# A hybrid RWKV-7 / gated-DeltaNet block: triangular inverses transposed into their own tile, the last of their loads requested first, and scan operands in longer DRAM pieces

## The chip, the core and the metric

One NeuronCore of a Trainium2 chip runs the whole two-layer network in one launch. The time is what the device takes for one execution, in microseconds (us). The kernel before took 3481.66 us (median of three runs, 3479.96 to 3486.83). The engines are called as in the profile: PE (TensorE matmul), PEld (its weight load), DVE (VectorE), ACT (ScalarE), POOL (GpSimd) and SP (SyncE). SP computes nothing in this kernel; it issues nearly all loads, one after the other.

## The reference

Float32 throughout. Layer 0 mixes tokens with two recurrences, each run forward and backward over 256 context and 1024 latent tokens:

```python
def _rwkv_scan(state0, r, decay, k, v, kk, b):      # 8 heads of 64
    def step(state, inp):
        r_t, w_t, k_t, v_t, kk_t, b_t = inp
        sa = jnp.einsum('bhij,bhj->bhi', state, kk_t)
        state = (state * w_t[:, :, None, :] - sa[..., None] * b_t[:, :, None, :]
                 + v_t[..., None] * k_t[:, :, None, :])
        return state, jnp.einsum('bhij,bhj->bhi', state, r_t)
...
def _gdn_chunked(state0, q, k, v, g, beta):         # 4 heads of 128, chunks of 64
    l_mat = jnp.where(strict, jnp.einsum('nbhid,nbhjd->nbhij', k_beta, kc) * decay, 0.0)
    sol = lax.linalg.triangular_solve(l_mat, rhs, left_side=True, lower=True, unit_diagonal=True)
    a_intra = jnp.where(incl, jnp.einsum('nbhid,nbhjd->nbhij', qc, kc) * decay, 0.0)
    def step(state, inp):
        q_i, k_i, u_i, w_i, g_i, a_i = inp
        v_new = u_i - jnp.einsum('bhlk,bhkv->bhlv', w_i, state)
        ...
```

Then come the output projection, an expert-choice mixture of experts, a layer of windowed attention, a second mixture of experts and a norm. The change touches the two recurrences and what prepares them.

## The kernel before, in words

Both recurrences are computed in 20 chunks of 64 tokens (`NCH`), two directions at once, by the same method: within a chunk a 64x64 unit lower triangular matrix is inverted, and a state is carried from chunk to chunk. There are 12 units: 0 to 3 are RWKV head pairs forward, 4 to 7 backward, 8 to 11 the DeltaNet heads.

**Preparation.** `InProj.run` multiplies the tokens by the input weights, one 128-column block after another. Each block's weights (`wraw`, two buffers) come through SP and are split into a high and a low part by ACT and POOL (`wlo`). Between the matmuls generators are stepped that prepare the operands. `Rwkv.prep_gen` forms, per block of 256 or 512 tokens and direction, the decayed arrays alpha, rho, beta and kappa in tile `arbk` and stores them as `s_rk`; `chunk_L` multiplies them to the triangular matrices and stores `s_L`; `vt` is the value array (`s_v`). `Gdn` does the same with a convolution (`convu`, DVE line L702), normalised k and q (`kqn` and `kqf`, stored as `s_kq`), decay matrices (`la`, stored as `s_L` and `s_At`) and token rows (`tok`, stored as `s_kv`). All these stores are issued by POOL. The order of these instructions on each engine is made by a scheduler that follows priorities; the generators of the inverses get a raised one (`tfill`).

**Inverses.** `tri_inv` loads 32x32 diagonal blocks into tile `invB`, one block per partition, and runs 31 elimination steps of two DVE instructions each (L852 `invt`, L853 `invX`). ACT writes the transpose into another tile, `invXT`, of the same two buffers, and both forms are stored as `s_T`. Eight such chains run one after the other. The seventh (96 partitions: the later chunks of unit 9 and the first four of units 10 and 11) ends the preparation, and the scan cannot form its first corner before it is stored. The eighth (units 10 and 11, chunks 4 to 19) runs inside the scan.

**Scan.** `Scan.run` has one step per chunk n. Here PE, DVE and POOL follow the order in which the code is written (`ORDER`): `rwkv` (ps_u, ps_U, ps_S, state S), `gdn` (ps_ks, ps_qs, ps_Y, ps_Sg), `corner(n+1)` (ps_p: the off-diagonal 32x32 corner of each inverse, from the tiles `t1`, `TT` and `l21`) and `gram(n+1)`. The loads are `load2` once per two chunks (tiles ar, bk, kq in both directions: 14 DMAs on SP), `load_tri(n+2)` (l21, t1 and four parts of TT: 6 DMAs) at the head of step n, and `load_tok(n+2)` (sv 4, at 1, and a gather of kv on POOL) at its end. SP works them off in that order. At the end of step 6 (`LATER`) `load_raw` requests the output weights `wo_raw`, 8 DMAs of 512 KB. Chain 8 is stepped once per letter of `ORDER`, so it fills DVE in steps 0 and 1.

The runs of consecutive bytes in the DRAM arrays are short: ar, the second half of bk and sv are loaded in pieces of 256 bytes, the first half of bk and kq in pieces of 512, and t1, TT and l21 in pieces of 128. The row of at is already one piece of 1 KB.

## Time and profile before

| | before |
|---|---|
| median of three runs | 3481.66 us |
| the profiled execution | 3488.81 us |
| its span, first to last instruction | 3487.0 us |
| mean granted TensorE clock | 0.945 of full speed |
| busy in the span: PE, DVE, ACT, POOL | 3127.7, 2438.2, 2074.6, 726.7 us |

The profiled execution is 7.15 us above the median, and 1.8 us of it lie outside the span. Shares over the whole span say little about this change: it touches the stretch from about 180 us (the first `arbk`) to 1224 us (the last output of the scan). The preparation's last projection matmul ends at about 807 us; the scan's steps run from about 842 to 1224 us. A wait row names the instruction that waited and what released it; an SP row gives when a DMA was issued and how long the issue held SP.

### The profile page before, as it was taken

To read this page: it belongs to the slowest core of one execution; us is meant where nothing else is said; L and a number is where in the kernel's file an instruction comes from. 1 tells how busy PE (TensorE), PEld (TensorE's weight loads), DVE (VectorE), ACT (ScalarE), POOL (GpSimd) and SP (SyncE) were. 2 spreads that over 40 slices of the span, in tenths; PEclk is the share of its full clock that TensorE was granted. 3 is DMA by queue.
4 is the path that set the end of the run, shared out by engine and by line. 5 is a ranking of instruction groups with operands and counts; after the bars stand their busy time and mean duration, and the time that the engine had idled before them with its cause. 6 is when DMAs were issued, how large, how long until landed. Compare 5 with 4: busy or idle time off the path is not lost. (4 is left out here: it accounts for less than half of the span.)

```text
span 3487.0 us, 60267 instructions
## 1 busy us (share of the span) xinstructions
PE 3127.7 (90%) x23392; PEld 2393.5 (69%) x23392; DVE 2438.2 (70%) x4066; ACT 2074.6 (59%) x3548; POOL 726.7 (21%) x716
## 2 busy tenths in 40 slices
PE   5999899995879878699999999799699958999997
PEld 3866667775768757567666767467577746888885
DVE  4268884666534457877777777634876787999998
ACT  4255454332434455477777667534688838888886
POOL 1133332222333343201111110011233310010101
PEclk9999999897889989799999999899899979999998
DMA  5256656666999765578888887662311058999995
GB/s 194 75 181 197 191 194 201 204 187 123 202 221 199 169 218 169 187 254 298 299 286 282 307 287 283 221 212 95 83 49 49 34 205 303 395 384 392 386 380 208
DMA packets 480161, 767.80 MB, mean 220 GB/s; under 512 B 231836, under 2 KB 318532, under 8 KB 472708
## 3 DMA queue, kind: packets, MB, share of 16 engines
q1 hardware_dynamic: 434640, 601.05, 51.5%
q0 software_dynamic: 41648, 151.55, 13.9%
q10 hardware_dynamic: 3587, 11.36, 1.1%
q8 instruction: 184, 3.01, 0.4%
q14 instruction: 102, 0.83, 0.1%
HBM read 631.48 MB, written 132.38 MB: 219 GB/s over the span
## 5 line engine op out<-in xcount | busy, mean ns | idle before, releaser
L1223 DVE TENSOR_TENSOR ulo<-raw,uhi 128x1024 fp32r<-128x1024 f32 x768 | 898.0, 1219 | 84.1 <-ACT uhi L1222 69.7
L1222 ACT ACTIVATE uhi<-raw 128x1024 fp32r<-128x1024 f32 x768 | 790.6, 1073 | 196.6 <-PE ps_y L1662 89.2
L1611 PE MATMUL ps_h<-uhi,xh 128*128 128x512 f32 x1024 | 329.0, 399 | 2.1 <-ACT uhi L1222 2.0
L1611 PE MATMUL ps_h<-ulo,xh 128*128 128x512 f32 x1024 | 319.3, 392 | 3.7 <-DVE ulo L1223 3.0
L1611 PE MATMUL ps_h<-uhi,xl 128*128 128x512 f32 x1024 | 318.6, 392 | 0.0
L1678 POOL DMA_INDIRECT s_x<-yo,idxl x31 | 49.2, 1588 | 945.0 <-DVE yo L1674 945.0
L1611 PEld LDWEIGHTS ps_h<-ulo,xh 128*128 128x128 f32 x1024 | 190.4, 188 | 53.9 <-DVE ulo L1223 12.7
L1611 PEld LDWEIGHTS ps_h<-uhi,xh 128*128 128x128 f32 x1024 | 186.2, 188 | 51.0 <-ACT uhi L1222 8.7
L1611 PEld LDWEIGHTS ps_h<-uhi,xl 128*128 128x128 f32 x1024 | 191.2, 188 | 40.6
L354 PE MATMUL ps_in<-hl,whi 128*128 128x512 f32 x512 | 173.0, 411 | 0.0
L354 PE MATMUL ps_in<-hh,whi 128*128 128x512 f32 x512 | 172.4, 413 | 0.0
L354 PE MATMUL ps_in<-hh,wlo 128*128 128x512 f32 x512 | 171.9, 410 | 0.0
L1662 PE MATMUL ps_y<-uhi,th 128*128 128x512 f32 x512 | 162.1, 397 | 0.7 <-ACT tc L1648 0.6
L1662 PE MATMUL ps_y<-ulo,th 128*128 128x512 f32 x512 | 159.9, 393 | 0.1
L1662 PE MATMUL ps_y<-uhi,tl 128*128 128x512 f32 x512 | 158.1, 390 | 0.0
L1584 ACT ACTIVATE xv<-ps_x,Gf 128x128 f32<-128x128 f32 x256 | 96.9, 471 | 67.0 <-PE ps_x L1580 67.0
L1962 POOL TENSOR_SCALAR pe<-pe,ast 128x640 f32<-128x640 f32 (+1 forms) x48 | 90.2, 1879 | 185.9 <-DVE ast L1961 88.0
L1976 PE MATMUL ps_pT<-ident,pe 128*128 128x128 f32 x608 | 95.9, 282 | 35.1 <-ACT pT L1980 17.2
L852 DVE TENSOR_TENSOR invt<-invB,invX 128x112 f32<-128x112 f32 (+27 forms) x248 | 102.0, 411 | 29.9 <-DMA invB<-s_L 24.6
L1662 PEld LDWEIGHTS ps_y<-uhi,th 128*128 128x128 f32 x512 | 93.7, 188 | 38.9 <-ACT uhi L1222 12.0
L1949 DVE CUSTOM_DVE_ANT_0 pe<-ps_s,amask,sink 128x640 f32<-128x640 f32 (+2 forms) x128 | 103.4, 809 | 24.2 <-PE ps_s L1942 22.8
L1617 PE MATMUL ps_hc<-raw,xc 128*32 128x512 f32 x1024 | 119.6, 596 | 0.0
(505 smaller groups left out, 7276.7 us busy)
## 6 DMA issues: line engine op xcount, KB each, us to landing
raw<-in_moe_w_dram SPq DMA_DIRECT2D x384, 1024.0 KB
ada_w<-in_ada_w_dram SPq DMA_DIRECT2D x48, 1024.0 KB
wraw<-in_e_w_in_dram SPq DMA_DIRECT2D x32, 512.0 KB
s_rk<-arbk POOLq DMA_DIRECT2D x16, 1024.0 KB, 5.2
kq<-s_kq SPq DMA_DIRECT2D x20, 512.0 KB
s_x<-ox POOLq DMA_DIRECT2D x18, 512.0 KB, 3.0
s_h<-ot POOLq DMA_DIRECT2D x18, 512.0 KB, 3.9
s_rkv<-rkv POOLq DMA_DIRECT2D x12, 640.0 KB, 3.9
```

The costliest lines, as they stand in the source:

```text
L354: nc.tensor.matmul(ps, l[:, k, :], r[:, k, a:a + m], start=(k == 0 and n == 0), stop=(k == 7 and n == 2))
L852: nc.vector.tensor_mul(t, B[:N, k, k + 1:, None].to_broadcast([N, r, c]), X[:N, k, None, 0:c].to_broadcast([N, r, c]))
L1222: K.nc.scalar.activation(hi, src, AF.Copy)
L1223: K.nc.vector.tensor_sub(lo, src, hi)
L1584: nc.scalar.activation(v[:, q], pt[:, q], AF.Identity, bias=self.nrm[:, 1, k, 0:1], scale=self.nrm[:, 0, k, 0:1])
L1611: nc.tensor.matmul(pl[m][n], l[:, k], r[:, 512 * n:512 * n + 512], start=(k == 0 and i == 0), stop=(k == 7 and i == 2))
L1617: nc.tensor.matmul(pc[32 * g:32 * g + 32], xc[:, k_], rs[g // 2][:, 512 * (g % 2):512 * (g % 2) + 512], start=(k_ == 0), stop=(k_ == 7), s ...
L1662: nc.tensor.matmul(py[n], l[:, k], r[:, 512 * n:512 * n + 512], start=(k == 0 and i == 0), stop=(k == 7 and i == 2))
L1678: nc.gpsimd.indirect_dma_start(out=K.s_x[1], out_offset=bass.IndirectOffsetOnAxis(ap=idx[:, e:e + 1], axis=0), in_=yo, in_offset=None, com ...
L1949: nc.vector.tensor_tensor_reduce(pe[:, a:b], sc[:, 512 - nl + a:512 - nl + b], self.mask[:, m:m + b - a], 1.0, low, OP.add, OP.min, st[:, ...
L1962: (nc.vector if n < NV else nc.gpsimd).tensor_scalar(pes[0][:, :nk], pes[0][:, :nk], st[:, 4, 0:1], None, op0=OP.mult)
L1976: nc.tensor.transpose(pt[:, k, i_], pes[i_][:, 128 * (c + k):128 * (c + k) + 128], K.ident)
```

## The change

- `tri_inv`: the transpose goes into the chain's own `invB` tile (`XT = B`) and no longer into a second buffer, so the next chain's `invB` has the other buffer.
- The eighth chain's generator is stepped once before `Scan` is built, so its `invB` loads stand ahead of all scan loads; `run` then steps it once where it stepped it twice.
- `s_rk` becomes (10, 128, 4, 512), with alpha and rho of two chunks first and beta and kappa after them: ar loads in pieces of 512 bytes, the first half of bk in pieces of 1 KB, the second half stays at 256 bytes. `s_kq` becomes (10, 128, 4, 2, 128): kq loads in pieces of 4 KB, and is stored with 16 DMAs in pieces of 512 bytes where it was 8 in pieces of 10 KB. `s_v` is ordered by head parity: sv loads with 2 DMAs in pieces of 1 KB where it was 4, and is stored with 24 DMAs in pieces of 256 bytes where it was 12 in pieces of 512. DVE forms kd first and then turns `av` in place into (av + 1) kk; the count of its instructions is unchanged.
- `wo_raw`: one of its 8 DMAs at the end of each of the steps 6 to 13.

```diff
@@ -539,22 +540,28 @@
-                x = wk.tile([128, 8, 4, 64], F32, name="arbk", tag="arbk", bufs=2)
+                x = wk.tile([128, 4, 512], F32, name="arbk", tag="arbk", bufs=2)
...
-                    return ap.rearrange("p (c t) -> p c t", t=64)
-                al, rh, be, ka = (x[:, :n, i] for i in range(4))
-                nc.vector.scalar_tensor_tensor(be, N3(av[:, :m]), 1.0, N3(kk[:, :m]), op0=OP.add, op1=OP.mult)
-                nc.vector.tensor_scalar(av[:, :m], av[:, :m], P("ka", ct), self.tka[:, ct:ct + 1],
+                    return ap.rearrange("p (m c t) -> p m c t", c=2, t=64)
...
+                def E4(sl):
+                    return E[:, :n, sl].rearrange("p (m c) t -> p m c t", c=2)
...
+                x1, x2 = (x[:, :n // 2, i:i + 256] for i in (0, 256))
+                al, rh = (x1.rearrange("p m (s c t) -> p m s c t", c=2, t=64)[:, :, i] for i in range(2))
+                be, ka = (x2.rearrange("p m (c s t) -> p m s c t", c=2, t=64)[:, :, i] for i in range(2))
+                kd = wk.tile([128, 512], F32, name="kd", tag="kd", bufs=2)
+                nc.vector.tensor_scalar(kd[:, :m], av[:, :m], P("ka", ct), self.tka[:, ct:ct + 1],
...
-                kd = wk.tile([128, 512], F32, name="kd", tag="kd", bufs=2)
-                nc.vector.tensor_mul(kd[:, :m], av[:, :m], k)
+                nc.vector.tensor_mul(kd[:, :m], kd[:, :m], k)
+                nc.vector.scalar_tensor_tensor(av[:, :m], av[:, :m], 1.0, kk[:, :m], op0=OP.add, op1=OP.mult)
...
-                nc.vector.tensor_mul(al, E[:, :n, exc], N3(kk[:, :m]))
-                nc.vector.tensor_mul(be, be, N3(iE[:, :m]))
-                nc.vector.tensor_mul(rh, E[:, :n, inc], N3(r))
+                nc.vector.tensor_mul(al, E4(exc), N3(kk[:, :m]))
+                nc.vector.tensor_mul(be, N3(av[:, :m]), N3(iE[:, :m]))
+                nc.vector.tensor_mul(rh, E4(inc), N3(r))
@@ -562,8 +569,8 @@
-                                    x[:, :n].rearrange("p (m c) s t -> p m (c s t)", c=2))
+                                    x[:, :n // 2])
@@ -592,8 +599,9 @@
-            nc.gpsimd.dma_start(dap(K.s_v, a * 512 + ct * 128, [[512, 128], [128 * 512, q], [1, 128]]),
-                                vt.rearrange("p (q i) -> p q i", i=128)[:, :q])
+            for h in range(2):
+                nc.gpsimd.dma_start(dap(K.s_v, a * 512 + h * 256 + ct * 64, [[512, 128], [128 * 512, q], [1, 64]]),
+                                    vt.rearrange("p (q h i) -> p h q i", h=2, i=64)[:, h, :q])
@@ -726,7 +734,9 @@
-                    nc.gpsimd.dma_start(dap(K.s_kq[d], h * 2 * T, [[8 * T, 128], [1, 2 * T]]), x.rearrange("p s t -> p (s t)"))
+                    for q in range(2):
+                        nc.gpsimd.dma_start(dap(K.s_kq[d], h * 256 + q * 128, [[1024, 128], [128 * 1024, 10], [1, 128]]),
+                                            x[:, q].rearrange("p (m t) -> p m t", t=128))
@@ -852,7 +862,7 @@
-    XT = wk.tile([128, 32, 32], F32, name="invXT", tag="invB", bufs=bufs)
+    XT = B
@@ -925,18 +935,20 @@
-            def v(p0, np_, arr, n=64):
-                return dap(K.s_rk[d], (mm * 128 + p0) * 2048 + arr * 64, [[2048, np_], [256, 8], [1, n]])
+            def v(p0, np_, o, n):
+                return dap(K.s_rk[d], (mm * 128 + p0) * 2048 + o, [[2048, np_], [512, 4], [1, n]])
...
-                return x.rearrange("p c k t -> p (c k) t")
-            nc.sync.dma_start(w(ar[0:64, 0]), v(0, 64, 0))
-            nc.sync.dma_start(w(ar[64:128, 1]), v(64, 64, 0))
-            nc.sync.dma_start(w(ar[:, 2]), v(0, 128, 1))
-            nc.sync.dma_start(bk[0:64].rearrange("p c k s t -> p (c k) (s t)"), v(0, 64, 2, 128))
+                return x.rearrange("p c k t -> p c (k t)")
+            nc.sync.dma_start(w(ar[0:64, 0]), v(0, 64, 0, 128))
+            nc.sync.dma_start(w(ar[64:128, 1]), v(64, 64, 0, 128))
+            nc.sync.dma_start(w(ar[:, 2]), v(0, 128, 128, 128))
+            nc.sync.dma_start(bk[0:64].rearrange("p c k s t -> p c (k s t)"), v(0, 64, 256, 256))
...
-                nc.sync.dma_start(w(bk[64:128, :, :, s]), v(64, 64, 3 - s))
-            nc.sync.dma_start(kq.rearrange("p h s t -> p (h s) t"), dap(K.s_kq[d], m * 128, [[8 * T, 128], [T, 8], [1, 128]]))
+                nc.sync.dma_start(bk[64:128, :, :, s].rearrange("p c k t -> p (c k) t"),
+                                  dap(K.s_rk[d], (mm * 128 + 64) * 2048 + 256 + 64 * (1 - s),
+                                      [[2048, 64], [512, 4], [128, 2], [1, 64]]))
+            nc.sync.dma_start(kq.rearrange("p h s t -> p (h s t)"), dap(K.s_kq[d], m * 128 * 1024, [[1024, 128], [1, 1024]]))
@@ -962,14 +974,13 @@
-            for d in range(2):
-                m = step_of(n) if d else n
-                nc.sync.dma_start(sv[r, hp, 4 * d:4 * d + 4], dap(K.s_v, 64 * m * 512 + hp * 64, [[512, 64], [128, 4], [1, 64]]))
+            nc.sync.dma_start(sv[r, hp].rearrange("p (d c) t -> p d (c t)", d=2),
+                              dap(K.s_v, 64 * n * 512 + hp * 256, [[512, 64], [64 * 512 * (step_of(n) - n), 2], [1, 256]]))
@@ -1181,7 +1192,7 @@
-        tri.step(2)
+        tri.step()
@@ -1206,8 +1217,8 @@
-            if n == LATER:
-                later(self.last)
+            if LATER <= n < LATER + 8:
+                later(n - LATER, self.last)
@@ -1323,10 +1334,9 @@
-def load_raw(K, t, W, last):
...
-    for k in range(8):
-        behind(K, K.nc.sync.dma_start(t[:, k], rows_ap(W, 128 * k * D, 128, D)), last.ins.name)
+def load_raw(K, t, W, k, last):
...
+    behind(K, K.nc.sync.dma_start(t[:, k], rows_ap(W, 128 * k * D, 128, D)), last.ins.name)
@@ -2126,11 +2136,11 @@
-        K.s_rk = [dt(f"s_rk{d}", (10, 128, 4, 2, 4, 64)) for d in range(2)]
+        K.s_rk = [dt(f"s_rk{d}", (10, 128, 4, 512)) for d in range(2)]
...
-        K.s_kq = [dt(f"s_kq{d}", (128, 4, 2, T)) for d in range(2)]
+        K.s_kq = [dt(f"s_kq{d}", (T // 128, 128, 4, 2, 128)) for d in range(2)]
@@ -2193,7 +2203,8 @@
-                Scan(K, sp, psg, psr, psn).run(lambda x: load_raw(K, wo, A["e_w_out"], x), tri)
+                tri.step()
+                Scan(K, sp, psg, psr, psn).run(lambda k, x: load_raw(K, wo, A["e_w_out"], k, x), tri)
```

SP at the change from preparation to scan, before: the loads of chunks 0 and 1 (sv, at, l, t, TT) and, behind them, chain 8's `invB`.

```order
L967 DMA sv<-s_v 64x4x64 x4
L972 DMA at<-s_At 128x256
L948 DMA l_6632<-s_L 128x12x32
L951 DMA t_6633<-s_T_165 128x12x32
L955 DMA TT_6635<-s_T_165 32x12x32 x4
L967 DMA sv<-s_v 64x4x64 x4
L972 DMA at<-s_At 128x256
L948 DMA l_6658<-s_L 128x12x32
L951 DMA t_6659<-s_T_165 128x12x32
L955 DMA TT_6661<-s_T_165 32x12x32 x4
L841 DMA invB<-s_L 32x32x32 x4
L948 DMA l_6847<-s_L 128x12x32
```

The same queue after, where the scan's loads begin; `wraw` and `ada_w` are weight loads of the preparation.

```order
L186 DMA ada_w<-in_ada_w_dram 128x2048 x5
L851 DMA invB<-s_L 8x32x32 x2
L186 DMA ada_w<-in_ada_w_dram 128x2048
L327 DMA wraw<-in_e_w_in_dram 128x8x128 x2
L851 DMA invB<-s_L 8x32x32 x2
L851 DMA invB<-s_L 32x32x32 x4
L943 DMA ar_6621<-s_rk_152 64x4x128
L944 DMA ar_6621<-s_rk_152 64x4x128
L945 DMA ar_6621<-s_rk_152 128x4x128
```

Chain 8's loads (32x32x32 x4) now stand ahead of the first ar load. Chain 7's (the 8x32x32 rows, and one 32x32x32 row further up) are spread between the weight loads; before, all six stood behind the last of these.

DVE near the end of the preparation, before: the last convolution (L702) among the steps of chain 7. The last number of L852 is the step's size, which rises to 256 at the middle of a chain and falls to 31 at its end.

```order
L702 SCALAR_TENSOR_TENSOR convu<-ps_inc,prm,convu 128x254
L853 TENSOR_TENSOR invX<-invX,invt 96x19x13
L702 SCALAR_TENSOR_TENSOR convu<-ps_in,prm,convu 128x1022
L852 TENSOR_TENSOR invt<-invB,invX 96x252
L702 SCALAR_TENSOR_TENSOR convu<-ps_in,prm,convu 128x1023
L853 TENSOR_TENSOR invX<-invX,invt 96x18x14
L702 SCALAR_TENSOR_TENSOR convu<-ps_in,prm,convu 128x1023
L852 TENSOR_TENSOR invt<-invB,invX 96x255
L702 SCALAR_TENSOR_TENSOR convu<-ps_in,prm,convu 128x1022
L853 TENSOR_TENSOR invX<-invX,invt 96x17x15
L852 TENSOR_TENSOR invt<-invB,invX 96x256
```

The same convolution after (L710), with what follows it up to the scan's first DVE instruction (L1012, in the old file L1001).

```order
L710 SCALAR_TENSOR_TENSOR convu<-ps_inc,prm,convu 128x254
L862 TENSOR_TENSOR invt<-invB,invX 96x60
L710 SCALAR_TENSOR_TENSOR convu<-ps_in,prm,convu 128x1022
L863 TENSOR_TENSOR invX<-invX,invt 96x2x30
L710 SCALAR_TENSOR_TENSOR convu<-ps_in,prm,convu 128x1023
L862 TENSOR_TENSOR invt<-invB,invX 96x31
L710 SCALAR_TENSOR_TENSOR convu<-ps_in,prm,convu 128x1023
L863 TENSOR_TENSOR invX<-invX,invt 96x31
L710 SCALAR_TENSOR_TENSOR convu<-ps_in,prm,convu 128x1022
L781 TENSOR_TENSOR tok<-ps_tk,vsc 128x512 x2
L781 TENSOR_TENSOR tok<-ps_tk,vsc 128x256
L1012 TENSOR_TENSOR ar_6621<-ps_g,strict 64x4x64
```

Before, chain 7 is at its middle when the last convolution ends, and 30 of its instructions follow before L1001; now the chain ends among the convolution's instructions, and only tok stands between them and the scan.

SP at step 6 of the scan, before, and then after.

```order
L972 DMA at<-s_At 128x256
L1329 DMA wo_raw<-in_e_w_out_dram 128x1024 x8
L948 DMA l_8910<-s_L 128x12x32
L951 DMA t_8911<-s_T_166 128x12x32
L955 DMA TT_6635<-s_T_166 32x12x32 x4
L967 DMA sv<-s_v 64x4x64 x4
L972 DMA at<-s_At 128x256
L948 DMA l_9193<-s_L 128x12x32
```

```order
L983 DMA at<-s_At 128x256
L1339 DMA wo_raw<-in_e_w_out_dram 128x1024
L960 DMA l_8897<-s_L 128x12x32
L963 DMA t_8898<-s_T_166 128x12x32
L967 DMA TT_6651<-s_T_166 32x12x32 x4
L977 DMA sv<-s_v 64x2x256 x2
L983 DMA at<-s_At 128x256
L1339 DMA wo_raw<-in_e_w_out_dram 128x1024
L960 DMA l_9179<-s_L 128x12x32
```

One `wo_raw` load instead of eight stands ahead of the l, t and TT of chunk 9, and sv has two DMAs in place of four.

## Rows read from the trace of the kernel before

**Rows 1.** Busy time by stretch: PE, PEld, DVE, ACT, POOL (instructions), clock, DMA share, GB/s.
```profile
230.00:807.00 577.00, 546.70 (x3497) 404.46 (x3497) 408.37 (x814) 259.06 (x346) 173.43 (x212) 0.93 0.62 195
807.00:842.00 35.00, 14.41 (x141) 11.75 (x140) 28.84 (x71) 7.13 (x8) 13.37 (x30) 0.66 0.39 95
...
898.00:1195.00 297.00, 254.07 (x5925) 225.88 (x5924) 129.87 (x283) 133.22 (x320) 105.30 (x97) 0.94 0.95 208
```

**Rows 2.** SP's queue around scan step 7: start, time it held SP, load.
```profile
995.60 6.13 SPq L1329 DMA_DIRECT2D wo_raw<-in_e_w_out_dram  x8
1001.77 0.50 SPq L948 DMA_DIRECT2D l<-s_L  x1
1003.65 7.65 SPq L951 DMA_DIRECT2D t<-s_T  x1
1011.35 4.93 SPq L955 DMA_DIRECT2D TT<-s_T  x4
```

**Rows 3.** What PE waited for from 842 to 1200: total us, times, longest.
```profile
PE ps_p L1024 <- DMA t<-s_T: 12.8, 2, 12.3
```

**Rows 4.** Timeline of DVE: the state update of steps 2, 3, 7, 8 and 18.
```profile
902.37 0.69 DVE L1088 TENSOR_TENSOR S<-ps_S,S 128x512 f32<-128x512 f32 x1 [5.05 <-PE ps_S L1079]
...
918.52 0.69 DVE L1088 TENSOR_TENSOR S<-ps_S,S 128x512 f32<-128x512 f32 x1 [3.22 <-PE ps_S L1079]
...
989.71 0.69 DVE L1088 TENSOR_TENSOR S<-ps_S,S 128x512 f32<-128x512 f32 x1 [4.75 <-PE ps_S L1079]
...
1020.43 0.69 DVE L1088 TENSOR_TENSOR S<-ps_S,S 128x512 f32<-128x512 f32 x1 [17.91 <-PE ps_S L1079]
...
1203.88 0.69 DVE L1088 TENSOR_TENSOR S<-ps_S,S 128x512 f32<-128x512 f32 x1 [5.28 <-PE ps_S L1079]
```

**Rows 5.** DMA queues from 898 to 1195: packets, MB, share of 16 engines' time.
```profile
q1 hardware_dynamic: 165566, 44.10, 76.1%
q0 software_dynamic: 5128, 16.79, 17.6%
```

**Rows 6.** The same of 3100 to 3400, where expert weights come in large pieces.
```profile
q1 hardware_dynamic: 27983, 107.90, 90.8%
```

**Rows 7.** The same of 545 to 570, in the preparation.
```profile
q1 hardware_dynamic: 4486, 1.96, 27.9%
```

**Rows 8.** Chain 7 from 807 to 830.4: DVE busy (instructions), ACT, POOL, clock, DMA share, GB/s.
```profile
807.00:830.40 23.40, 14.94 (x43) 0.00 (x0) 0.00 (x0) 0.60 0.20 48
```

**Rows 9.** Timeline of DVE there: last convolution's first and last instruction, first scan instruction.
```profile
807.82 0.47 DVE L702 SCALAR_TENSOR_TENSOR convu<-ps_inc,prm,convu 128x254 f32<-128x254 f32 x1
...
815.24 1.27 DVE L702 SCALAR_TENSOR_TENSOR convu<-ps_in,prm,convu 128x1022 f32<-128x1022 f32 x1
...
830.41 0.43 DVE L1001 TENSOR_TENSOR ar<-ps_g,strict 64x256 f32<-64x256 f32 x1
```

**Rows 10.** SP's queue at the scan's start.
```profile
827.70 0.38 SPq L948 DMA_DIRECT2D l<-s_L  x1
837.26 0.37 SPq L951 DMA_DIRECT2D t<-s_T  x1
...
850.92 2.77 SPq L841 DMA_DIRECT2D invB<-s_L  x4
```

**Rows 11.** Timeline of PE and DVE in step 0 of the scan.
```profile
853.06 1.98 PE L1079 MATMUL ps_S<-sv,bkt 128*64 128x64 f32 x32
...
858.93 0.19 DVE L852 TENSOR_TENSOR invt<-invB,invX 128x31 f32<-128x31 f32 x1 [16.98 <-DMA invB<-s_L]
...
860.99 0.68 DVE L1086 TENSOR_TENSOR S<-ps_S,PC 128x512 f32<-128x512 f32 x1
```

**Rows 12.** POOL's store groups by form: busy us, mean ns | idle before.
```profile
L729 POOL DMA_DIRECT2D s_kq<-kqn x4 | 2.3, 578 | 7.2 <-ACT kqn L720 7.2
```

**Rows 13.** What SP waited for from 230 to 860: total us, times, longest.
```profile
SPq L327 <- POOL wlo L338: 189.4, 13, 29.6
...
SPq L841 <- DMA s_L<-Lt: 31.7, 3, 18.1
```

More of the change, by code (lines that the diff above doesn't have):

```diff
@@ L451, in invert, with chunk_L @@
         yield
-    def chunk_L(self, ct, d, x, n0, n):
+    def chunk_L(self, ct, d, al, be, n0, n):
         K, nc = self.K, self.K.nc
@@ L459, in chunk_L @@
                 hr = slice(64 * h, 64 * h + 64)
-                nc.tensor.matmul(pl[hr, 64 * cc:64 * cc + 64], x[hr, cc, 0 if d else 2], x[hr, cc, 2 if d else 0],
+                l, r = al[hr, cc // 2, cc % 2], be[hr, cc // 2, cc % 2]
+                nc.tensor.matmul(pl[hr, 64 * cc:64 * cc + 64], l if d else r, r if d else l,
                                  start=True, stop=True, skip_group_check=True)
@@ L564, in prep_gen @@
                                         [[2048, 128], [128 * 2048, n // 2], [1, 512]]),
-                                    x[:, :n].rearrange("p (m c) s t -> p m (c s t)", c=2))
-                late.append(self.chunk_L(ct, d, x, n0, n))
+                                    x[:, :n // 2])
+                late.append(self.chunk_L(ct, d, al, be, n0, n))
                 yield
@@ L971, in load_tok @@
                                      in_offset=bass.IndirectOffsetOnAxis(ap=self.rows[:, n:n + 1], axis=0))
-        nc.sync.dma_start(at, dap(K.s_At, n * 128 * 256, [[256, 128], [64, 4], [1, 64]]))
+        nc.sync.dma_start(at.rearrange("p h t -> p (h t)"), dap(K.s_At, n * 128 * 256, [[256, 128], [1, 256]]))
         self.tok[n] = (sv, kv, at)
```

## The prediction

> **What bounds the kernel now.** I read busy time by stretch first. From 230 to 807 us PE is busy 546.70 of 577 us, with a DMA share of 0.62: the preparation is bound by PE, and a change to its stores or loads moves it only if PE is made to wait. From 807 to 842 PE is busy 14.41 of 35 and DVE 28.84: the tail is a chain of DVE work. From 898 to 1195, steps 2 to 18 of the scan, PE is busy 254.07 of 297 while the DMA engines are busy 0.95 of the time [rows 1]. So in the scan the loads come first, which two more views bear out. In SP's queue the 8 output-weight loads go out at 995.60, l, t and TT of the next chunk stand behind them, and t holds SP for 7.65 us [rows 2]; PE waits 12.3 us on that t [rows 3]. The state updates on DVE give the beat: 16.15 us from step 2 to step 3 (the shortest gap), 30.72 from step 7 to 8 (the stall), and 1203.88 - 902.37 = 301.5 us for all 16 gaps, 18.84 each [rows 4].
>
> What fills the DMA engines is pieces, not bytes. In that stretch SP's queue moved 165,566 packets and 44.10 MB and took 76.1% of 16 engines [rows 5]: 0.761 x 297 x 16 / 165,566 = 21.8 ns for a piece of 266 bytes. Where expert weights stream it moved 27,983 packets and 107.90 MB at 90.8% [rows 6]: 155.7 ns for 3,856 bytes, at most 40 ns per 1,000 bytes. The bytes of a scan piece are thus worth 266 x 0.0404 = 10.8 ns, and the other 11 ns belong to the piece itself. A stretch of the preparation, with less contention, gives 111.6 us / 4,486 = 24.9 ns for 437 bytes [rows 7], by which a piece costs only 24.9 - 17.7 = 7.2 ns. I take 11, since it comes from the stretch in question, and keep 7.2.
>
> **The change part by part.**
>
> *Layouts, loads.* By the code, `load2` issues 9,216 pieces per two chunks and 4,864 after; `load_tok` 1,152 per chunk and 384 after; `load_tri` stays at 4,608. The stretch holds 8 `load2` and 15 of the others: 8 x 9,216 + 15 x 5,760 + 1,024 (output weights) = 161,152, against 165,566 in the trace, so the count is about right. After, it is 8 x 4,864 + 15 x 4,992 + 1,024 = 114,816. The 46,336 pieces saved are worth 46,336 x 11 / 16 = 31.9 us of all 16 engines (20.9 at 7.2 ns).
>
> By a sentence of the Trainium skill, "DMA: Bandwidth & Descriptors", section "Why small descriptors are slow (HBM only)", each packet carries a fixed overhead of about 3 cycles, 3 of 11 for a descriptor of 256 bytes. By that, 27% of the 21.8 ns, 5.9 ns, would be the piece's own (an estimate from that page and the row), and the saving 46,336 x 5.9 / 16 = 17 us in place of 31.9, which gives 15 us more time than my sum. The trace can't split the 21.8 ns further than the two lines above do.
>
> *Output weights.* One per step in place of 8 at once removes the wait of 12.3 us [rows 3] as such. Their bytes remain, and with a DMA share of 0.95 the stall was only where the debt of the queue was paid in one piece. So I don't add 12.3 to the saving: together, the two edits let the 16 gaps shrink by what the queue saves, 32 us, less some 4 because PE's and the loads' needs will no longer lie in one fixed order within a step: -28. Bounds: if the loads saved nothing and only the stall went, between 0 and -17 (12.3 and the slower steps around it); if PE's pace of the shortest gap held everywhere, 16 x 16.15 = 258.4, that is -43.
>
> *Scan start.* Chain 7 has 43 DVE instructions of 14.94 us after 807 [rows 8]; the last convolution runs there from 807.82 to 816.5, and the scan's first DVE instruction starts at 830.41 [rows 9]. SP issues l at 827.70, after the last token store, and t at 837.26, after the inverse is stored [rows 10]. After the change chain 7 is all but through when the convolution ends (its loads no longer stand behind the last weights, and the next chain need not wait for the buffer that held the transpose), so t can go out straight behind l: 837.26 becomes about 828.5. What is late next is the token rows' store, which l waits for now. I take -8.5; bounds -5 (the token rows slip a little) and -9.5 (t issued with l).
>
> *Step 0.* DVE stands 16.98 us until 858.93, since chain 8's `invB` loads go out at 850.92, behind the loads of two chunks [rows 10, 11]. ps_S had ended at 853.06 + 1.98 = 855.04, yet the update of S came at 860.99 [rows 11]. With the loads ahead of all scan loads S can follow ps_S at once: 860.99 - 855.04 = 5.95, less the dispatch: -5.5; bounds 0 (chain 8 must be worked off by DVE anyway, and then steps 1 and 2 are longer) and -6.
>
> *Stores.* POOL needs 578 ns for one s_kq store whatever its pieces [rows 12]. There are 8 more s_kq and 12 more s_v DMAs, 20 x 0.58 to 0.75 = 12 to 15 us on an engine busy 173 of 577 [rows 1]. Their pieces: s_kq goes from a few hundred long ones to 20,480, 20,480 x 11 / 16 = 14 us of DMA, s_v adds 5,120, 3.5 us. The idle 38% of the DMA engines, 219 us, hides them: 0. If that cover is gone (a store late where a load waits for it) up to +10; -5 if kq's pieces, now written in the order in which they are read, land sooner.
>
> *The hoisted `invB` loads.* They stand among the weight loads of the preparation, in SP's order. SP waited for `wraw`'s buffers 13 times, 189.4 us in all, 14.6 each [rows 13]: that is its slack before a weight is wanted, and it hides one issue of 1 to 3 us: 0. The form of DVE's `arbk` instructions changes, their number and size not: 0.
>
> *Sum.* -8.5 - 5.5 - 28 + 0 = -42. The profiled execution took 3488.81 (span 3487.0 and 1.8 outside), 7.15 above the median; 3488.81 - 42 = 3446.8, and less 7.15 it is 3440 as a median. The main case's own range, from -14 - 17 = -31 (7.2 ns a piece, with the 4 us lost) to -9.5 - 6 - 32 - 5 = -52, is 3429 to 3451.
>
> **The rivals.**
>
> *PE sets the pace.* With 28% of the scan's pieces gone, loads stop binding and each gap falls to 16.15, as from step 2 to 3 [rows 4]: -43 - 14 = -57, 3425. For it: PE needs 254.07 of 297 [rows 1], so there is room. Against: that gap came when the loads of two chunks were already in, and the pieces of 128 bytes, 15 x 4,608 or three fifths of what is left, stay.
>
> *Time goes with bytes.* If the 21.8 ns are mostly waiting for memory under contention, fewer pieces with the same bytes save little: 10 us in the steps, with the spread output weights 0 to 20, and -14 before them: -24, 3458. For it: 7.2 ns in a calm stretch [rows 7]; against: [rows 5, 6], where the large pieces move 2.4 times the bytes at a similar share. The overhead that the Trainium skill's page (cited above, same section) states would put the time at 3455, in this case's reach.
>
> *No gain before step 1.* Token stores, not t, hold the scan's start, and step 1 gives back what step 0 gains: -28, 3454. Against: t's 837.26 is 9.6 us behind l [rows 10].
>
> *The hoisted loads hold SP (slower).* An `invB` load must wait until the matrices of its units are stored; SP waited so 3 times, up to 18.1 us [rows 13], at the end, where nothing stood behind it. Now weights stand behind it. A wait of 18.1 less the slack of about 10 left of the 14.6 makes PE idle 8 us; over 7 chains +56, against -42: +14, 3496. It decides from 6 us per chain on. Against: in all of the preparation these loads made SP wait but 31.7 us, and the matrices of chains 1 to 6 are stored well before 807.
>
> *Nothing to be seen.* The saving is taken up by stores and queueing: within 0.2% of 3481.66, about 7 us, which is about what a measurement of this kernel can tell from no change: 3475 to 3489.
>
> **How the numbers follow.** Main case 0.40, PE's pace 0.20, bytes 0.20, no gain before step 1 0.08, SP held 0.07, nothing 0.05. Faster by over 0.2%: 0.40 + 0.20 + 0.20 + 0.08 = 0.88; same 0.05; slower 0.07. The prediction is the main case, 3440. The range reaches from just below PE's pace (3420) to the middle of the bytes case and its neighbour's upper half (3466), and leaves out the last two cases and part of the third.
>
> **What the profile after would show.** If the steps are right: gaps between updates of S of 16.9 to 17.1 us, none of 30; no wait of PE's ps_p on t above 4 us; some 46,000 packets fewer in the same 16 gaps, and at their shares less than 0.95 of DMA; SP with idle gaps in the scan. For the scan's start: its first DVE instruction near 822, t issued near 828.5, right behind l. For step 0: no DVE wait of 17 us on `invB`. For the stores: PE as busy from 230 to 807 as before, and the last projection matmul still at 807. I am wrong if PE waits for `wraw` in the preparation (SP held), if the DMA share stays at 0.95 with the pieces gone (bytes), if the gaps fall to 16.2 (PE's pace), or if l moves later than 830 (stores).

## The result, and the profile after

| | before | after |
|---|---|---|
| median | 3480.81 us (4 runs, 3476.8 to 3486.83) | 3516.73 us (4 runs, 3507.2 to 3529.15) |
| profiled execution, span | 3488.81, 3487.0 us | 3509.64, 3507.8 us |
| last projection matmul ends | 807.3 us | 856.9 us |
| first update of S (step 0) | 861.0 us | 896.2 us |
| from there to the S of step 18 | 342.9 us | 332.1 us |
| from there to the end | 2283.2 us | 2279.5 us |

The changed kernel is slower: the ratio of the times is 1.0105 (95% interval 1.0087 to 1.0124). The medians differ by 35.9 us and the two profiled spans by 20.8, since the profiled execution of before lies 8.0 above its median and that of after 7.1 below. The table can split only the 20.8: 49.6 lost up to the last projection, 53.7 - 39.3 = 14.4 won back from there to the first S, 10.8 won in the scan, 3.7 behind it. So the loss lies in the preparation, which the prediction had booked at nothing, and the scan's gain is a third of the 28 forecast.

Busy time of the changed kernel by stretch (columns as in [rows 1]; the last is steps 2 to 18 at their new place):

```profile
230.00:807.00 577.00, 516.20 (x3251) 373.37 (x3251) 374.82 (x767) 249.71 (x336) 191.33 (x216) 0.91 0.59 185
...
931.00:1228.00 297.00, 258.27 (x6156) 232.86 (x6152) 132.68 (x292) 136.72 (x329) 111.36 (x101) 0.94 0.93 215
```

PE is busy 516.2 of the 577 us where it was 546.7 [rows 1]: it lost 30 us of work there. One wait of PE between 470 and 600 us carries most of it, and SP's waits in the preparation say why (columns: total us, times, longest):

```profile
PE ps_inc L354 <- ACT whi L337: 25.6, 1, 25.6
```

```profile
SPq L327 <- POOL wlo L338: 101.3, 11, 19.7
SPq L851 <- DMA s_L<-Lt: 80.1, 7, 37.3
SPq L851 <- DMA s_L<-la: 57.5, 7, 28.7
...
SPq L327 <- DMA s_T<-invX: 40.0, 1, 40.0
```

SP waited 31.7 us for the stores of s_L before [rows 13], and 80.1 + 57.5 now. The 40.0 us is a weight load (L327) that waited for the store of an inverse, which it does not read; before, such waits came to 1.7 us. SP's queue there (start, time it held SP), and ACT's timeline:

```profile
444.47 16.14 SPq L327 DMA_DIRECT2D wraw<-in_e_w_in_dram  x2
498.07 18.59 SPq L851 DMA_DIRECT2D invB<-s_L  x20
556.77 1.84 SPq L327 DMA_DIRECT2D wraw<-in_e_w_in_dram  x2
```

```profile
549.81 1.96 ACT L866 ACTIVATE invB<-invX 128x1024 f32<-128x1024 f32 x1
551.79 2.57 ACTq L876 DMA_DIRECT2D s_T<-invB  x2
554.40 1.87 ACTq L876 DMA_DIRECT2D s_T<-invX  x1
562.42 1.06 ACT L337 ACTIVATE whi<-wraw 128x1024 fp32r<-128x1024 f32 x1 [10.66 <-DMA wraw<-in_e_w_in_dram]
```

Read them as a chain of events. The 20 `invB` loads of chains 4 and 5 wait until 498 for s_L; chain 4 runs on DVE and is transposed at 549.81; the weight load behind them goes out at 556.77, `whi` follows at 562.42, PE at 563.5. Before, this weight load (the 23rd) went out at 495.29. In the trace's records it waits on a completion counter (102, one of the eight, 100 to 107, that SP's and ACT's DMAs use), and the DMA before it on that counter is chain 4's store, issued at 549.38. In ACT's order before, the 23rd and 24th `whi` stood ahead of chain 4's transpose; now the transpose stands ahead of both:

```profile
512.89 1.05 ACT L337 ACTIVATE whi<-wraw 128x1024 fp32r<-128x1024 f32 x1
...
529.33 1.05 ACT L337 ACTIVATE whi<-wraw 128x1024 fp32r<-128x1024 f32 x1
...
546.40 2.04 ACT L856 ACTIVATE invXT<-invX 128x1024 f32<-128x1024 f32 x1
```

PE's clock adds to it (granted clock is the last column but two):

```profile
537.30:563.50 26.20, 0.66 (x4) 0.22 (x2) 15.03 (x41) 8.40 (x8) 3.00 (x4) 0.59 0.65 170
563.50:569.30 5.80, 5.77 (x15) 4.38 (x16) 4.58 (x5) 4.73 (x8) 4.81 (x2) 0.50 0.42 110
```

PE stood still for 25.6 us, the clock fell to the lower of its two levels, 1.2 GHz, and stayed there for the first 5.8 us of work. From 160 us to the last projection the mean granted clock is 0.912 (0.939 before), and PE is idle 70.7 us (36.1) and busy 626.2 (611.2): of what was lost up to there, two thirds are idle time and the rest is work that took longer.

In the scan the queues' row can be held against [rows 5]:

```profile
q1 hardware_dynamic: 123520, 44.97, 72.5%
```

A quarter of the pieces is gone (165,566 to 123,520), the bytes are nearly the same, and SP's queue still takes 72.5% of 16 engines: 0.725 x 297 x 16 / 123,520 = 27.9 ns for 364 bytes, where it was 21.8 ns for 266. Two points on one line: 0.062 ns a byte and 5.3 ns a piece. The records of single packets agree: in the scan before, the mean is 13.9 ns for 128 bytes, 21.7 for 256, 36.4 for 512 and 68.7 for 1 KB.

### The profile page after: what moved, and what is told of

Same layout as the page of the kernel before. It is cut to its first block, busy times and chain, and to the rows that moved or that the text cites. A ratio compares the mean times of both kernels' runs of the same rounds, so it can differ in the third digit from the quotient of the medians.

```text
span 3507.8 us, 60236 instructions
## 1 busy us (share of the span) xinstructions
PE 3133.3 (89%) x23392; PEld 2395.1 (68%) x23392; DVE 2429.3 (69%) x4066; ACT 2074.2 (59%) x3547; POOL 757.1 (22%) x736
## 3 DMA queue, kind: packets, MB, share of 16 engines
q0 software_dynamic: 43504, 151.55, 13.9%
## 5 line engine op out<-in xcount | busy, mean ns | idle before, releaser
L1621 PEld LDWEIGHTS ps_h<-ulo,xh 128*128 128x128 f32 x1024 | 190.6, 188 | 53.6 <-DVE ulo L1234 12.4
L1393 PE MATMUL ps_out<-woh,mh 128*128 128x512 f32 x288 | 116.3, 449 | 0.0
```

Source lines behind the costliest of these rows:

```text
L1393: nc.tensor.matmul(po[:, cp_], l, r[:, k, c_], start=(k == 0 and n == 0), stop=(k == 7 and n == 2))
L1621: nc.tensor.matmul(pl[m][n], l[:, k], r[:, 512 * n:512 * n + 512], start=(k == 0 and i == 0), stop=(k == 7 and i == 2))
```

## The experiments

Each kernel is one edit of the kernel before or after. "S" is the update of the state in step 0; "scan" is from there to the S of step 18. Single profiles of equal programs differ. e7 has the preparation of the kernel before, and its S is 2.4 us earlier; the eight profiles with the changed kernel's scan (after, e1, e3, e4, e9 to e12) give 329.8 to 338.6 us for it, three of the old scan (before, e2, e8) 342.9 to 344.6. So by themselves a few us of S, and up to some 9 us of the scan, show nothing. The ratios (against the kernel before, with 95% intervals) are from timed runs.

| run | last projection | S | scan | ratio |
|---|---|---|---|---|
| before | 807.3 | 861.0 | 342.9 | |
| after | 856.9 | 896.2 | 332.1 | 1.0105 (1.0087 to 1.0124) |
| e1 own tile | 828.2 | 872.6 | 329.8 | 1.0007 (0.9993 to 1.0022) |
| e2 in place alone | 839.5 | 884.0 | 344.6 | 1.0095 (1.0062 to 1.0129) |
| e3 one buffer | 829.2 | 896.8 | 338.0 | 1.0117 (1.0088 to 1.0146) |
| e4 stores on POOL | 849.9 | 893.0 | 332.5 | 1.0079 (1.0053 to 1.0104) |
| e5 layouts alone | 820.8 | 872.1 | 327.6 | 1.0003 (0.9986 to 1.0019) |
| e6 early loads alone | 803.9 | 851.4 | 341.6 | 0.9981 (0.9966 to 0.9996) |
| e7 spread weights alone | 806.0 | 858.6 | 343.0 | 1.0007 (0.9990 to 1.0024) |
| e8 third buffer | 814.8 | 859.0 | 344.6 | 1.0021 (1.0005 to 1.0036) |
| e9 no priority | 838.9 | 878.8 | 332.7 | 1.0049 (1.0032 to 1.0065) |
| e10 kd on ACT | 822.4 | 866.1 | 338.6 | 1.0006 (0.9995 to 1.0017) |
| e11 transposes held back | 820.9 | 863.8 | 332.7 | 0.9975 (0.9964 to 0.9986) |
| e12 chain 5's loads held back | 835.6 | 875.3 | 331.6 | 1.0018 (1.0003 to 1.0033) |
| e13 rk layout alone | 817.2 | 870.3 | 339.7 | 1.0040 (1.0024 to 1.0056) |
| e14 kq and v layouts alone | 812.9 | 863.7 | 333.0 | 1.0002 (0.9989 to 1.0016) |
| e15 best, in place | 804.0 | 842.5 | 329.1 | 0.9938 (0.9919 to 0.9958) |
| e16 best, own tile | 824.0 | 869.4 | 329.8 | 0.9976 (0.9963 to 0.9990) |

### Is it XT = B? (e1, e2)

e1, on the changed kernel (e2 is the reverse edit on the kernel before):

```diff
-    XT = B
+    XT = wk.tile([128, 32, 32], F32, name="invXT", tag="invB", bufs=bufs)
```

> The changed kernel with one part undone: the transpose goes into a second tile again, so the invB loads of chains 2 to 7 fall back to their old places. Theory (hoisted invB loads hold SP, and the weight loads behind them come late): the first update of S falls from 896 us to about 856 to 865, PE's longest wait for whi from 25.6 to under 5, the scan from first to last S stays at 332; total about 3465, 0.5% below before. Rival (the new stores and layouts slow the preparation): the first S stays near 890, total near 3510.

> The kernel before with one part of the change alone: XT = B. Theory (hoisted invB loads hold SP): first update of S at 885 to 900 (861 before), SP waits of 30 us or more at invB and at the wraw load behind it, scan from first to last S unchanged at 343; total 3505 to 3525. Rival (stores and layouts slow the preparation): first S at 850 to 861, total 3470 to 3482.

One line costs 23.0 us of S on the kernel before (861.0 to 884.0) and 23.6 on the changed one (872.6 to 896.2). PE's 25.6 us for `whi` is gone in e1; e2 has a wait of 13.7 us at the same block. But e1's S stays at 872.6 where 856 to 865 was expected: some 11 us of the loss are not XT = B, and the total is 3482 and not 3465. In the timed runs e2 alone (1.0095) is nearly as slow as the whole change (1.0105).

### What about it? (e3, e4, e8, e9)

```diff
e3  -    B = wk.tile(..., name="invB", tag="invB", bufs=bufs)
e3  +    B = wk.tile(..., name="invB", tag="invB", bufs=1)
e4  -    (chains 1 to 6) store = nc.scalar.dma_start
e4  +    (chains 1 to 6) store = nc.gpsimd.dma_start
e8  -    invX: bufs=bufs;  invXT: tag="invB", bufs=bufs
e8  +    invX: bufs=1;     invXT: tag="invT", bufs=1
e9  -    fill, tfill = Fill(tc, 1200), Fill(tc, 600)
e9  +    fill, tfill = Fill(tc, 1200), Fill(tc, 0)
```

> The changed kernel with one invB buffer in place of two: a chain's loads then wait for the store of the chain before, as late as in the kernel before or a little later, with the transpose still in place. In this program no wraw load waits for the store of an inverse. Theory (hoisting, not the transposing in place, costs the time): first S at 850 to 870, no wait of PE for whi over 5 us; total 3455 to 3475. Rival (a chain without a spare buffer starts too late and ends the preparation later): first S at 875 or more, total 3490 or more.

Half right. The preparation is as short as e1's (829.2 against 828.2) and no wait for `whi` over 5 us is left, so transposing in place costs nothing that shows here. But chain 7 now waits for its only buffer, ends at 875, and PE waits 29.2 us at the scan's start: the rival's S and total.

> The changed kernel with the stores of the inverses of chains 1 to 6 issued by POOL in place of ACT; invB loads stay hoisted. Two waits of SP stand ahead of the 23rd weight load: 37.3 us at invB for the store of s_L, then 40.0 us at wraw for the store of an inverse that ACT issues, which it does not read. Theory A (the second wait is the one that costs: wraw shares a completion counter with that store): the second wait goes, the load is issued near 517 in place of 557, PE's wait of 25.6 us for whi is gone, first S at 860 to 872, total 3475 to 3490. Theory B (the first wait, SP's order alone, costs it): first S stays at 885 to 900, total 3505 to 3525.

Theory B's numbers, and not its mechanism. The 40 us at the weight load are gone (it went out at 521.73), yet S is 893.0 and the total 3507. ACT's timeline of e4 shows the next queue in line:

```profile
541.91 2.04 ACT L866 ACTIVATE invB<-invX 128x1024 f32<-128x1024 f32 x1 [0.55 <-DVE invX L863]
543.85 0.46 ACT L307 ACTIVATE convu<-ps_inc,prm 128x256 f32<-128x256 f32 x1
...
551.20 1.27 ACT L728 ACTIVATE kqn<-convu 128x1280 f32<-128x1280 f32 x1 [2.09 <-DVE invt L862]
...
554.62 1.99 ACT L337 ACTIVATE whi<-wraw 128x1024 fp32r<-128x1024 f32 x2
```

The weights are there, but `whi` stands in ACT's order behind chain 4's transpose, and behind a `kqn` whose input (`convu`) DVE makes between chains 4 and 5. PE waits 12.4 us. The shared counter was one link of several: what is ordered behind the end of chain 4 waits for it, here on ACT and DVE.

> The kernel before, not transposing in place, but with a buffer of its own for the transpose (and one invX in place of two, to make room): a chain's invB loads may then go out as early as in the changed kernel. On SP they stand nearly where XT = B puts them (chain 5's 16 loads behind the 24th weight block, behind the 22nd with XT = B, behind the 26th before; chain 7's spread over the 29th to 32nd). Theory (what costs is that the loads and steps of the chains stand earlier in the in-order queues, not the transposing in place): first S at 875 to 895 (861 before, 884 with XT = B alone), total 3495 to 3515. Rival (the transpose into the tile that DVE has just read, and the store that then holds this tile, cost it): first S at 855 to 868, total 3475 to 3487.

My theory of that moment, early places on SP, is not borne out: the loads stand early, SP waits 120.7 us for stores of s_L (31.7 before, 137.6 in the changed kernel), and still S is 859.0 and the total, 3485, within the rival's range. With one `invX`, chain 4's transpose stands behind the 25th `whi` (24th before, 22nd with XT = B). That points to the place of a chain's end and not of its loads; as chain 5's loads stand two weight blocks later than with XT = B, this run alone does not decide it.

> The changed kernel with the chains' raised priority taken away (the lead of tfill 0 in place of 600); transposes stay in place. Chain 5's loads then stand behind the 24th weight block (22nd in the changed kernel), chain 6's behind the 29th (26th), the rest a little later. Theory (the early places of the chains cost it): PE's idle time from 160 us to the last projection falls from 70.8 to 50 to 60 us, first S from 896 to 870 to 885, total 3485 to 3500. Rival (no link with the places): first S within 5 us of 896, total near 3515. It can also end the preparation later if chain 7 is late: then the first S is late while the last projection is early.

As the theory said, and only part of the cost goes: the transpose of chain 4 moves behind the 23rd `whi`, S to 878.8.

### The places put back, transpose still in place (e11, e12)

```diff
e11 -    nc.scalar.activation(XT[:N], X[:N]..., AF.Copy)
e11 +    i = nc.scalar.activation(XT[:N], X[:N]..., AF.Copy)
e11 +    behind(K, i, K.whi[act - 1])      # act = 24, 28, 31 for chains 4, 5, 6
e12 +    behind(K, i, K.wraw[26 - 1])      # i: each invB load of chain 5
```

In both runs the chains concerned are also written into the program only once that many `whi` stand in it.

> The changed kernel with one order added on ACT: the transposes of chains 4, 5 and 6 may not stand ahead of the 24th, 28th and 31st whi, where they stood before (22nd, 24th and 28th in the changed kernel); transposes stay in place. The chains' steps on DVE and loads on SP follow: chain 5's loads fall back behind the 26th weight block. Theory (XT = B lets the planner put chain 4's end ahead of the 23rd weight block; on the chip its input lands only near 495 us, and what stands behind its end in an in-order queue waits): no PE wait over 8 us for whi, PE idle from 160 us to the last projection 43 to 52 us (70.8), last projection at 822 to 835 (857), first S at 860 to 875 (896), total 3472 to 3485. Rival (transposing in place costs by itself): first S at 885 or more, total 3500 or more.

> The changed kernel with one order added on SP: chain 5's 16 invB loads behind the 26th weight load, where they stood before (22nd in the changed kernel). Chain 4's transpose then stands behind 23 whi (22 in the changed kernel, 24 before). Theory of the lane and of the places: part of the cost goes, first S at 865 to 882, total 3478 to 3492. Rival (chain 5 has no part in it): first S within 6 us of 896, total 3508 or more.

e11 settles that the transposing in place is not what costs, but the order that comes with it. With the places of three transposes on ACT put back, and with them chain 5's loads (behind the 26th and 27th weight load), S goes from 896.2 to 863.8, the ratio from 1.0105 to 0.9975, and the stretch reads

```profile
230.00:807.00 577.00, 538.92 (x3452) 396.49 (x3451) 401.01 (x829) 267.33 (x354) 202.31 (x228) 0.93 0.64 194
```

```profile
525.95 1.06 ACT L338 ACTIVATE whi<-wraw 128x1024 fp32r<-128x1024 f32 x1 [3.54 <-issue]
557.26 1.06 ACT L338 ACTIVATE whi<-wraw 128x1024 fp32r<-128x1024 f32 x1 [2.39 <-PE ps_in L355]
558.89 2.13 ACT L874 ACTIVATE invB<-invX 128x1024 f32<-128x1024 f32 x1
```

The 23rd and 24th `whi` stand ahead of chain 4's transpose again, and PE has no wait over 2.5 us between 470 and 600. DVE starts chain 4 at 515, later than in the changed kernel (509): its input sets that, since SP waits 37.8 us for s_L ahead of its loads, as in the changed kernel (37.3). e12 puts chain 5's loads back, chain 4's transpose moves by one `whi`, and two thirds are won (S 875.3).

Over the runs S goes with the place of chain 4's transpose: behind the 22nd `whi` 884.0 to 896.2 (e2, e4, after), behind the 23rd 875.3 and 878.8 (e12, e9), behind the 24th or 25th 842.5 to 872.6 (all others but e3, where chain 7 is late). Between e9 and e12, with the same place, chain 5's loads move from mostly the 24th to the 26th weight load and S by 3.5 us. No run moves the transposes and leaves all loads where XT = B puts them, so how the cost divides between ACT's order and SP's is not shown.

### The layouts (e5, e10, e13, e14)

e5 takes the hunks on s_rk, s_kq and s_v from the change; e13 those on s_rk alone, e14 those on s_kq and s_v. e10 is e1 with

```diff
-                nc.vector.tensor_scalar(kd[:, :m], av[:, :m], P("ka", ct), self.tka[:, ct:ct + 1],
-                                        op0=OP.mult, op1=OP.add)
+                nc.scalar.activation(kd[:, :m], av[:, :m], AF.Identity, scale=P("ka", ct), bias=self.tka[:, ct:ct + 1])
```

> The kernel before with the longer DRAM pieces alone (s_rk, s_kq, s_v, their stores and loads). By the packets of the two traces, one of 128 bytes takes 13.9 ns, of 256 bytes 21.7, of 512 bytes 36.4, of 1 KB 68.7: some 6 ns a piece and the rest with the bytes. Theory (time goes with bytes): the scan from first to last S gets 5 to 12 us shorter (343 before), total 3468 to 3478. Rival (my 11 ns a piece): 25 to 30 us shorter, total near 3452. The preparation: first S within 10 us of 861 if the many short stores are hidden, above 870 if they are not.

> The changed kernel with the transpose in its own tile (as in the first experiment), and the first step of kd (av times ka plus a constant) on ACT in place of DVE. In the runs with the new layouts 3 to 5 of these 24 DVE instructions lay beside a wlo of POOL: they took 2.4 to 2.7 us in place of 0.54, and that wlo 3.2 to 5.1 us in place of 2.4; none did so before. Theory (this meeting is what the layouts cost in the preparation): no wlo above 3.1 us, PE's waits for arbk fall from 26.0 to about 18 us, first S from 872.6 to 862 or less; with the scan at 328 to 332 from first to last S the total is 3462 to 3472. Rival (the stores cost it): first S stays at 870 or more, total 3478 to 3485.

> The kernel before with the s_rk layout alone (ar and bk in longer pieces; the new order of DVE's steps for kd). By the packet times it saves, per two chunks, 4,096 pieces of 256 bytes for 2,048 of 512 and 512 of 512 for 256 of 1 KB: 4,096 x 21.7 - 2,048 x 35.4 + 512 x 36.4 - 256 x 66 = 18 us of one engine, 1.1 us of 16, 9 us over 8 pairs of chunks at most. Theory (the meeting of kd's first step with wlo costs the preparation): scan 334 to 338 from first to last S (343), first S 866 to 874. Rival (the stores cost it): first S 857 to 864.

> The kernel before with the s_kq and s_v layouts alone, loads and stores (20 more DMAs on POOL, in shorter pieces). Per two chunks 2,048 pieces of 512 bytes become 256 of 4 KB (2,048 x 36.4 - 256 x 233 = 15 us of one engine), and per chunk 1,024 of 256 become 256 of 1 KB (1,024 x 21.7 - 256 x 64 = 5.8 us): 1.7 us of 16 engines per two chunks, some 14 us in all at most. Theory (kd's meeting costs the preparation, not the stores): first S 857 to 865, scan 333 to 340, total 3468 to 3476. Rival (the stores cost it): first S 868 to 876, total 3477 or more.

e5: 15.3 us off the scan, more than the 5 to 12 expected, and 11.1 on S; over its ten timed runs nothing remains. e13 and e14 part them: with s_rk the scan is 3.2 us shorter, no more than equal scans differ, and S 9.3 later (ratio 1.0040); with s_kq and s_v the scan is 9.9 shorter and S 2.7 later, and the total, 3479 (ratio 1.0002), is not the 3468 to 3476 expected. The ratios do not add up: 1.0040 and 1.0002 apart, 1.0003 together. One difference in the preparation shows in two groups. First e13, then e14 (count | busy us, mean ns | idle before):

```profile
L338 POOL TENSOR_TENSOR wlo<-wraw,whi 128x1024 fp32r<-128x1024 f32 x24 | 72.1, 3004 | 39.1 <-ACT whi L337 39.0
...
L555 DVE TENSOR_SCALAR kd<-av,prm,pcols 128x512 f32<-128x512 f32 (+1 forms) x24 | 20.2, 850 | 6.5 <-ACT av L527 6.4
```

```profile
L338 POOL TENSOR_TENSOR wlo<-wraw,whi 128x1024 fp32r<-128x1024 f32 x24 | 59.1, 2468 | 20.2 <-ACT whi L337 19.4 <-issue 0.6
L731 POOL DMA_DIRECT2D s_kq<-kqn x8 | 7.8, 972 | 23.0 <-ACT kqn L721 23.0
...
L548 DVE TENSOR_SCALAR av<-av,prm,pcols 128x512 f32<-128x512 f32 (+1 forms) x24 | 11.8, 496 | 0.0
```

The mean of 850 ns is that of two kinds: 20 of the 24 take 0.40 to 0.58 us, and four take 2.36 to 2.67, those that lie for 2.2 to 2.3 us beside a `wlo`. As the first of its steps the instruction now comes straight after ACT's `av`; as the second it met no `wlo` at all. With that step on ACT (e10) S comes down by 6.5, PE's waits for `arbk` from 26.0 to 21.6, and one `wlo` of 5.9 us is left. But the total did not move (1.0006 after 1.0007), as the rival had it. So the meeting is shown; that it costs time is not. The kernel before has such meetings too: in its trace 19 DVE instructions, most of them steps of the chains, take 2.2 to 5.5 us beside a `wlo`, in e13's only 12. What is new in e13 is that `wlo` itself is held (91.3 us for all 32, 78.3 in e14). Why S comes 9 us later stays open.

### The other two parts (e6, e7)

> The kernel before with chain 8's invB loads alone ahead of the scan's. As predicted: step 0's wait of 17 us for invB goes, first S 5.5 us earlier (855), total 3475. Rival (chain 8 must be worked off by DVE all the same, and steps 1 and 2 give it back): first S earlier, the S of step 2 at 902 as before, total 3481.

> The kernel before with the output weights' loads alone spread over steps 6 to 13. If the wait of 12.3 us was the queue's debt paid at once: the gap of 30.7 us falls to some 18, others grow, the scan from first to last S stays within 3 us of 343, total 3479 to 3483. Rival (the stall was a loss of its own): 8 to 12 us shorter, total 3470.

e6 takes the `tri.step()` ahead of Scan alone: S comes 9.6 us earlier, 3.4 of it in the last projection already, whose program is the same, so that 6.2 are the part's own. Step 2 keeps the lead (890.8 against 902.4). e7 takes the spread `wo_raw` loads alone: the gap of 30.7 us from step 7 to 8 becomes 19.6, others grow (the longest but the first is 24.6, from step 9 to 10), and the scan is as long as before (343.0). The stall was debt: the queue's work, paid in one step.

### What the runs point to (e15, e16)

e16: the kernel before with the s_kq and s_v layouts and the early loads; e15: the same with XT = B and e11's order.

> What the runs point to: the kernel before with the s_kq and s_v layouts, chain 8's loads ahead of the scan's, XT = B with the transposes of chains 4 to 6 held behind the 24th, 28th and 31st whi; without the s_rk layout and with the output weights requested at once. Theory (the parts add up): first S 861 + 2.7 (kq, v) - 9.6 (early loads) - up to 8 (chain 7 ends earlier) = 846 to 855, scan 332 to 337 from first to last S, total 3460 to 3468. Rival (the places of the chains differ in every program, so parts do not add up): 3470 or more.

> The same without XT = B: the kernel before with the s_kq and s_v layouts and chain 8's loads ahead of the scan's. Theory (the parts add up): first S 861 + 2.7 - 9.6 = 854, scan 332 to 337, total 3464 to 3470. Rival (they do not add up): 3473 or more.

e15 is the fastest: 3457.32 us, ratio 0.9938, 24 us below the kernel before in the same series (3481.69). S is at 842.5, earlier than forecast: from the last projection to S it takes 38.5 us (53.7 before), the gain that the change meant chain 7 and chain 8's early loads to bring. e16's time is 3472, between the forecast and its rival; its S, 869.4, is 15 us later than the sum of its parts. So parts do not simply add up, upwards in e15 and downwards in e16. The cause is open: the chains of e16 stand where those of e14 stand (S 863.7), and PE idles no longer from 160 us to the last projection (44.3 us, e14 45.6), but is busy 12.4 us longer there, at a mean granted clock of 0.931 in place of 0.942.

## Why the prediction was wrong

- **The hoisted `invB` loads: 0, and a rival at 0.07.** This step failed. I hid their issue under SP's slack of 14.6 us at `wraw` [rows 13], and gave the rival 8 us for each of 7 chains. It was not a delay for every chain but mainly one place: chain 4's loads stand behind the 22nd or 23rd weight load in every run and can go out only near 491 to 501 us in before, after, e1 and e11, when their s_L is stored; the new order puts chain 4's end and chain 5's loads ahead of the 23rd weight block, and PE stood 25.6 us. My words against the rival, that those loads made SP wait but 31.7 us, took waits of an order that the change replaces. I also misread the longest of them. I put the 18.1 us at the end, where nothing stood behind them; in the trace of before all three waits lie between 230 and 500 us, and this one is chain 4's, with the 23rd weight load right behind it. The waits of SP from 440 to 500, and its queue there:

```profile
SPq L841 <- DMA s_L<-Lt: 18.1, 1, 18.1
```

```profile
491.27 3.44 SPq L841 DMA_DIRECT2D invB<-s_L  x4
495.29 8.33 SPq L327 DMA_DIRECT2D wraw<-in_e_w_in_dram  x2
```

  The rival's mechanism, SP alone, was too narrow as well (e4, e8); its total of 3496 was the nearest of all, and PE's wait for weights in the preparation, the sign that I had named for it, came.
- **Scan start: -8.5.** Right. As forecast, t goes out right behind l, 20.9 us behind the last projection where it was 30.0 (837.26 [rows 10] after 807.3): -9.1. The queue of the changed kernel:

```profile
877.21 0.43 SPq L960 DMA_DIRECT2D l<-s_L  x1
877.75 0.76 SPq L963 DMA_DIRECT2D t<-s_T  x1
```

  With step 0, from the last projection to S it takes 39.3 us and not 53.7, -14.4, and e15 keeps -15.2. It starts from a point that is 49.6 later.
- **Step 0: -5.5.** Right. From the issue of t to S it takes 18.5 us where it was 23.7, -5.3; e6 shows 6.2 behind the last projection, kept in steps 1 and 2.
- **Steps 2 to 18: -28.** Mis-sized: -8.8 in the profile after, -13.3 in e5. I split 21.8 ns into 11 for the piece and 10.8 for its bytes, taking the price of a byte from pieces of 3,856 bytes at a stretch of other loads [rows 6]. That the loads cost the steps was right: with fewer pieces the steps are shorter. The split is 5.3 and 16.5: 42,046 pieces x 5.3 / 16 = 13.9 us, less the same 4 about -10. The rule from the Trainium skill ("DMA: Bandwidth & Descriptors", "Why small descriptors are slow (HBM only)"), quoted ahead of the result with 5.9 ns and 17 us, was nearer than my own line, and so was the rival by bytes (10 us); its sign, a DMA share that stays near 0.95, came too (0.93). The two rows of the same kernel [rows 5, 7] could have warned me: the calmer one gave 7.2 ns.
- **Spread weights: no gain of their own.** Right (e7).
- **Stores: 0; `arbk`: 0, same number and size.** Wrong by about 11 us of S (e5), most of it with s_rk (e13), whose stores are as many and as long as before (0.75 us each). I put the new order of DVE's steps at nothing because their number and size stay; what of it costs the time is open. One store of s_kq holds POOL for 972 ns, not 578 "whatever its pieces"; e14, which has these stores, loses 2.7 us of S, about what equal preparations differ by.

## What to carry to other kernels

A buffer set free is a change of order: where a planner places work by estimated times, look at what now stands behind the freed work in each in-order queue, and when that work's input really lands in the trace of before. Price pieces against bytes from the same stretch, with two piece sizes, before counting on longer ones. When one part wins and another loses, time the parts apart: here the sum was 1.0% slower and a selection of the same parts, with three transposes put back to their places, 0.6% faster.

## What the runs showed of the hardware

- In e13 POOL's `wlo` (2.4 us by itself) and DVE held each other up in turn. Two rows of it:

```profile
406.16 5.12 POOL L338 TENSOR_TENSOR wlo<-wraw,whi 128x1024 fp32r<-128x1024 f32 x1 [0.73 <-ACT whi L337]
```

```profile
408.95 2.65 DVE L555 TENSOR_SCALAR kd<-av,prm,pcols 128x512 f32<-128x512 f32 x1
```

  The `wlo` starts while DVE works off five instructions without a gap, the last of which starts at 408.35. It takes 2.7 us more than by itself, and DVE's row of five lasts 2.9 us beyond its start. The next DVE instruction then takes 2.65 us in place of 0.54 and ends 0.3 us behind the `wlo`. The longest of e13's five `wlo` over 4 us, 7.85, met ten such instructions that lasted 5.6 us beyond its start. The Trainium skill, "SBUF — State Buffer", section "SBUF: two separate sides", says that DVE and GpSimd share one pair of ports under an exclusive lock; both waits agree with it.
- A store's issue on POOL went from 578 to 972 ns when its form changed from one long piece per partition to 10 pieces of 512 bytes ([rows 12], e14).
